# Softmax attention in one written-out order on TensorE, with the value products one step behind, rotation halves moved by DMA, and the merge's splits behind its first weights

## The chip, the cores and the metric

One Trainium2 chip, one core. Its engines run beside each other, each through its own instructions in a fixed order: TensorE (PE, matrix products), VectorE (DVE), ScalarE (ACT), GpSimd (POOL), and SyncE (SP), which issues most of the DMAs. The metric is the device time of one execution, in microseconds (us).

## The reference

Two blocks, for 512 tokens of width 1024 in fp32. The first holds two layers of feed-forward networks and token mixers. The second is one hybrid layer: from the normed input come softmax attention (8 query heads and 2 key/value heads of 128, over the 512 tokens and 256 context tokens), gated linear attention (GLA, in chunks), two sigmoid gates that merge the branches, and a squared-relu MLP. The part that the change is about:

```
qx = apply_rope(rms_norm_2(split_heads(aq, N_Q_HEADS, HEAD_DIM), q_norm), cos, sin)
kx = apply_rope(rms_norm_2(split_heads(ak, N_KV_HEADS, HEAD_DIM), k_norm), cos, sin)
...
s = jnp.einsum('bqhgd,bkhd->bhgqk', q_blk, k, preferred_element_type=jnp.float32) * (HEAD_DIM ** -0.5)
p = jax.nn.softmax(s, axis=-1).astype(v.dtype)
return jnp.einsum('bhgqk,bkhd->bqhgd', p, v)
...
y = jax.nn.sigmoid(gate_a) * (attn @ w_br_attn) + jax.nn.sigmoid(gate_g) * (gla @ w_br_gla)
return y @ w_out
```

## The kernel before

Activations lie with the features on the 128 partitions and the 512 tokens along the row. Every fp32 matrix is split into two parts that PE takes at full speed: `split` writes the high part with a cast on ACT (L182) and the low part with a subtraction on DVE (L183). A product is then three matmuls (`mm3`: low weights by high input L193, high by high L194, high by low L195). Weights come by SP's DMAs as tiles of 128 x 1024 (512 KB, `wraw`) and are split into `whi` and `wlo` just ahead of their use; in the attention there are three buffers of `wraw` and two each of `whi` and `wlo`. A projection (`proj`) is 8 such triples of 512 columns.

A scheduler orders the instructions of each engine ahead of time from its own model of time; what a buffer's last reader or writer was becomes a wait. Where the kernel marks a matmul with `pin`, its place among the marked ones is kept as written. Pools of buffers are shared by a tag: whoever takes a buffer next waits for its last user. In PSUM the attention has one buffer `pj` (projections), two `sc` of two banks each (scores), two `tp` (transposes and small sums) and one `po` (value products).

`attention_phase` follows the GLA. `query(hd)` projects one head, sums its squares over the features by matmuls (`token_sums`, PSUM name `qsum`), takes the reciprocal root on POOL, scales (`qf`), and rotates (`rotate`): four ACT copies of 32 x 512 (L1134) bring each quarter of the partitions to its partner's place (`sw`), and three DVE operations multiply by the tables and add. The two keys (`kraw`, made earlier) go the same way, their norm spread over the partitions by matmuls (`kR`). For each head and each half of the tokens come two query tiles: 6 score matmuls of 384 columns each, the maximum on DVE (L1104), its product with the norm (L1105), the exponential with its sum on ACT (L1106), the reciprocal (L1108) and the scaling (L1109) on DVE; then 12 transposes of 128 x 128 in three groups (L1117), each split into `PTh` and `PTl`; 18 value matmuls of 256 columns; and the split of their result into `ath` and `atl`. Between them stand projections for the merge's gates (`merge_gates`): the sigmoid is three ACT passes (L794 to L796), and the gate is kept in DRAM (`gsave`, L805, a DMA from ACT's queue). The scheduler alone decides how these mix, since of all this only the first matmul of a step is marked, and only in phases that use `run`.

`merge_phase` first loads the tokens' stream `x` from DRAM and scales it, splits all eight GLA heads (`gla` to `glh` and `gll`), then for 8 output tiles multiplies both branches with their weights and adds them under the gates.

Of the kernel before, what the change touches and what calls it, by code (L numbers as in the profile page):

```python
# [17 lines left out]
P = 128  # L18
D = 1024
KT = D // P  # L20
T = 512
# [127 lines left out]
class Builder:  # L149
# [554 lines left out]
    def run(self, steps):  # L704

        for step in steps:
            self.mark = True
            step()
        self.mark = False
# [87 lines left out]

    def merge_gates(self, n):
        for i in range(self.ngates, min(self.ngates + n, 2 * KT)):
            w = self.wm(self.gate_at(i))  # L800
            ps = self.psum("pj")
            self.proj(ps, w, self.hs)
            sg = self.ptmp.tile([P, T], F32, name="sg", tag="sq")
            self.sigmoid(sg, ps)
            self.nc.scalar.dma_start(self.gsave[i], sg)  # L805
            self.ngates = i + 1
# [225 lines left out]
    def attention_phase(self, ctx):  # L1032
# [7 lines left out]
        def query(hd):  # L1040
            w = self.wm(WM_AQ + hd)
            ps = self.psum("pj")
            self.proj(ps, w, self.hs)
            sq = self.ptmp.tile([P, T], F32, name="qsq", tag="sq")
            nc.scalar.activation(sq, ps, AF.Square)
            sums = self.psum("pj", "qsum")
            self.token_sums(sums, sq, 4)
            r = self.rstd(sums[:, 0:4], 4, P, "q")
            rs = self.psmall.tile([P, 4], F32, name="rs4")
            nc.vector.tensor_scalar(rs, r[:, 0:4], QSCALE, None, ALU.mult)  # L1050
            qf = p2.tile([P, T], F32, name="qf", tag="qf")
            nc.scalar.activation(qf, ps, AF.Copy, scale=self.vec("q_norm_2", 0, 1))
            qr = self.rotate(p2, qf)
            qh = p2.tile([P, T], F32R, name="qh", tag="qh")
            ql = p2.tile([P, T], F32R, name="ql", tag="ql")
            self.split(qh, ql, qr)
            return qh, ql, rs

        attn = []
        nxt = query(0)  # L1060
        for i in range(2):
            for n, at in ((C, T), (T, 0)):
                raw = self.kraw[i][:, at:at + n]
                sq = self.ptmp.tile([P, T], F32, name="ksq", tag="sq")[:, :n]
                nc.scalar.activation(sq, raw, AF.Square)
                sums = self.psum("tp", "ksum")
                self.token_sums(sums, sq, n // P)
                r = self.rstd(sums[:, :n // P], n // P, P, "k")
                R = self.psum("tp", "kR")
                self.spread(R, r, n // P)  # L1070
                kf = p2.tile([P, T], F32, name="kf", tag="qf")
                nc.scalar.activation(kf[:, :n], raw, AF.Copy, scale=self.vec("k_norm_2", 0, 1))
                if at == 0:
                    kf = self.rotate(p2, kf)
                kr = p2.tile([P, T], F32, name="kr", tag="kr", bufs=1)
                nc.vector.tensor_tensor(kr[:, :n], kf[:, :n], R[:, :n], ALU.mult)
                self.split(K[i][0][:, at:at + n], K[i][1][:, at:at + n], kr[:, :n])
        wv = [self.chunk(d["wv"][GH - 1, i]) for i in range(2)]
        self.values(wv, lambda tt, ps: self.split(Vh[:, tt], Vl[:, tt], ps), tags=("pj", "po"))
        for hd in range(8):  # L1080
            kv = hd // 4
            qh, ql, rs = nxt
            if hd < 7:
                nxt = query(hd + 1)
            oh = self.pah.tile([P, T], F32R, name=f"ath{hd}", tag=f"ah{hd}")
            ol = self.pal.tile([P, T], F32R, name=f"atl{hd}")
            for half in range(2):
                if hd and half == 0:
                    self.merge_gates(1)
                PT = [(p2.tile([P, 2, 256], F32R, name=f"PTh{i}", tag=f"PTh{i}"), p2.tile([P, 2, 256], F32R, name=f"PTl{i}", tag=f"PTl{i}"))  # L1090
                      for i in range(3)]
                probs = []
                for j in range(2):
                    qt = half * 2 + j
                    sl = slice(qt * P, (qt + 1) * P)
                    pr = p2.tile([P, 768], F32, name="probs", tag="probs", bufs=2)
                    mx = self.psmall.tile([P, 8], F32, name="mx")
                    sc = self.psum("sc", "sc", 1024).rearrange("p (e n) -> p e n", e=2)[:, :, 0:384]
                    for e in range(2):
# [170 lines left out]
```

## Time and profile before

| | |
|---|---|
| median of 3 runs | 2739.99 us (2739.67 to 2746.25) |
| the profiled execution, its own time | 2741.75 us |
| its span in the trace | 2740.0 us, 34603 instructions, mean granted clock of PE 0.997 |
| PE busy | 2698.5 us (98%), 14005 matmuls |
| DVE busy | 1532.5 us (56%) |
| ACT busy | 950.2 us (35%) |
| POOL busy | 36.1 us (1%) |
| DMA | 354.42 MB, mean 129 GB/s |

Each engine's busy time is the sum of its instructions; the share is that of the span. The execution's own time is the span and 1.75 us around it.

### The profile page before, as it was taken

Reading aid. Unit: us, or ns where it says so; the run is one execution under the profiler, and the core shown is the slowest. Engines: PE = TensorE matmul, PEld = TensorE weight load, DVE = VectorE, ACT = ScalarE, POOL = GpSimd, SP = SyncE. Lnnn points to the kernel's source line nnn. Section 1 sums busy time; section 2 is a strip of 40 time slices with the busy share of each in tenths; the row PEclk is TensorE's granted clock in tenths of the full one; section 3 lists DMA queues with packets and bytes.
Section 4 is the critical chain, followed back from the end, with each engine's and each line's share of the span. In section 5 each row is a group of like instructions: output and inputs, shape, how many; then the busy total and the mean of one; then the engine's idle time right before and its main releaser. Section 6 shows DMA issues by size and latency. Waiting matters only on the chain.

```text
span 2740.0 us, 34603 instructions
## 1 busy us (share of the span) xinstructions
PE 2698.5 (98%) x14005; PEld 2326.1 (85%) x14005; DVE 1532.5 (56%) x2499; ACT 950.2 (35%) x1474; POOL 36.1 (1%) x47
## 2 busy tenths in 40 slices
PE   7999999999999999999999999999999999999999
PEld 6888889888898888888988889899888888988887
DVE  7645567444466455754674555655446665554433
ACT  4222244222242222332432233644346652333322
POOL 0000000000000000000000000000000000000000
PEclk9999999999999999999999999999999999999999
DMA  8745543444536454433364542211221125233232
GB/s 333 246 146 185 186 138 125 145 135 135 165 114 212 138 177 150 135 100 97 111 223 138 170 146 71 89 55 47 66 85 55 51 70 176 89 100 100 93 100 78
DMA packets 102977, 354.42 MB, mean 129 GB/s; under 512 B 11424, under 2 KB 11680, under 8 KB 102688
## 3 DMA queue, kind: packets, MB, share of 16 engines
q1 hardware_dynamic: 100512, 348.00, 39.4%
q10 hardware_dynamic: 2304, 4.20, 0.4%
q8 instruction: 110, 1.80, 0.3%
q14 instruction: 51, 0.42, 0.0%
HBM read 343.76 MB, written 8.39 MB: 129 GB/s over the span
## 4 chain that ended last, share of the span: by engine, by line
PE 96%; DVE 1%; ACT 1%; DMA 1%; issue 0%; SPq 0%; POOL 0%; DVEq 0%; ACTq 0%
PE mm L193 29%; PE mm L194 29%; PE mm L195 29%; PE mm L1008 3%; PE mm L926 1%; PE mm L1014 1%; PE mm L1117 1%; ACT whi L182 0%; PE mm L446 0%; PE mm L492 0%; PE mm L479 0%; PE nR L273 0%; PE sc L1101 0%; PE sc L1103 0%; PE sc L1102 0%
## 5 line engine op out<-in xcount | busy, mean ns | idle before, releaser
L193 PE MATMUL mm<-hh,wlo 128*128 128x512 f32 (+1 forms) x2344 | 884.5, 379 | 3.2 <-ACT hh L289 1.8
L194 PE MATMUL mm<-hh,whi 128*128 128x512 f32 (+1 forms) x2344 | 878.7, 377 | 0.0
L195 PE MATMUL mm<-hl,whi 128*128 128x512 f32 (+1 forms) x2344 | 869.3, 377 | 0.4 <-DVE hl L290 0.3
L182 ACT CAST whi<-wraw 128x1024 fp32r<-128x1024 f32 (+1 forms) x443 | 456.7, 1034 | 921.6 <-PE mm L195 478.0
L183 DVE TENSOR_TENSOR wlo<-wraw,whi 128x1024 fp32r<-128x1024 f32 (+1 forms) x443 | 532.7, 1205 | 285.6 <-ACT whi L182 282.1
L193 PEld LDWEIGHTS mm<-hh,wlo 128*128 128x128 f32 x2344 | 442.8, 189 | 82.4 <-ACT hh L289 2.2
L194 PEld LDWEIGHTS mm<-hh,whi 128*128 128x128 f32 x2344 | 442.6, 189 | 77.7
L195 PEld LDWEIGHTS mm<-hl,whi 128*128 128x128 f32 x2344 | 437.4, 189 | 80.7 <-DVE hl L290 0.8
L194 PE MATMUL mm<-g,whi 128*128 128x512 f32 (+1 forms) x1147 | 416.1, 363 | 0.0
L193 PE MATMUL mm<-g,wlo 128*128 128x512 f32 (+1 forms) x1147 | 416.0, 363 | 0.0
L195 PE MATMUL mm<-g,whi 128*128 128x512 f32 (+1 forms) x1147 | 413.7, 362 | 0.0
L312 DVE SCALAR_TENSOR_TENSOR x<-mm,mod,x 128x512 f32<-128x512 f32 (+1 forms) x171 | 113.8, 666 | 319.8 <-PE mm L195 319.8
L193 PEld LDWEIGHTS mm<-g,wlo 128*128 128x128 f32 x1147 | 216.5, 189 | 33.6
L194 PEld LDWEIGHTS mm<-g,whi 128*128 128x128 f32 x1147 | 216.5, 189 | 33.5
L195 PEld LDWEIGHTS mm<-g,whi 128*128 128x128 f32 x1147 | 216.5, 189 | 33.4
L238 DVE SCALAR_TENSOR_TENSOR adaw<-adaw,cond 128x1024 f32<-128x1024 f32 x176 | 208.7, 1220 | 2.9 <-DMA adaw<-in_ada_dram 2.9
L351 DVE TENSOR_TENSOR gf<-sa,mm 128x512 f32<-128x512 f32 (+1 forms) x94 | 61.3, 653 | 197.6 <-PE mm L195 188.9
L350 ACT ACTIVATE sa<-mm 128x512 f32<-128x512 f32 (+1 forms) x94 | 53.6, 570 | 314.7 <-PE mm L195 314.7
L289 ACT ACTIVATE hh<-hn,mod 128x256 fp32r<-128x256 f32 (+1 forms) x120 | 57.9, 518 | 54.9 <-DVE hn L288 47.3
L257 DVE TENSOR_TENSOR nacc<-nacc,sq 128x256 f32<-128x256 f32 (+1 forms) x108 | 52.1, 486 | 32.5 <-ACT sq L256 31.9
L256 ACT ACTIVATE sq<-x 128x256 f32<-128x256 f32 (+1 forms) x90 | 42.0, 467 | 66.3 <-DVE x L312 64.0
L1199 DVE TENSOR_TENSOR rl<-rl 128x512 f32<-128x512 f32 (+1 forms) x36 | 22.5, 633 | 75.0 <-ACT rl L1198 74.8
(263 smaller groups left out, 2544.2 us busy)
## 6 DMA issues: line engine op xcount, KB each, us to landing
wraw<-in_ffn_in_dram SPq DMA_DIRECT2D x176, 512.0 KB, 3.5
adaw<-in_ada_dram SPq DMA_DIRECT2D x176, 512.0 KB, 4.7
wraw<-in_wm_dram SPq DMA_DIRECT2D x66, 512.0 KB, 3.7
wraw<-in_mlp_dram SPq DMA_DIRECT2D x64, 512.0 KB, 3.7
wraw<-in_ffn_out_dram SPq DMA_DIRECT2D x64, 448.0 KB, 3.4
wraw<-in_ffn_out_dram SPq DMA_DIRECT2D x32, 512.0 KB, 3.6
wraw<-in_conv_in_dram SPq DMA_DIRECT2D x24, 512.0 KB, 3.5
ads<-in_ada_dram SPq DMA_DIRECT2D x8, 512.0 KB, 10.4
```

Of the source, the lines that this page charges most:

```text
L182: self.nc.scalar.copy(hi, src)
L183: return self.nc.vector.tensor_tensor(lo, src, hi.bitcast(F32), ALU.subtract)
L193: self.pin(mm(ps, wlo, xhi, start=start, stop=False))
L194: mm(ps, whi, xhi, start=False, stop=False)
L195: mm(ps, whi, xlo, start=False, stop=stop)
L238: nc.vector.scalar_tensor_tensor(out, raw, 1.0, self.cond[:, cond], ALU.mult, ALU.mult, accum_out=dst)
L257: nc.vector.tensor_tensor(acc, acc, sq[:, :n], ALU.add)
L289: first = nc.scalar.activation(hi, u, AF.Identity, bias=sh[:, k:k + 1])
L312: self.nc.vector.scalar_tensor_tensor(x, ps[:, :seg[1]], gate[:, k:k + 1], x, ALU.mult, ALU.add)
L350: nc.scalar.activation(sa, pa[:, :seg[1]], AF.Silu)
L351: nc.vector.tensor_tensor(gf, sa, pb[:, :seg[1]], ALU.mult)
L1008: self.pin(mm(o, (xl, xh, xh)[n][:, t0:t0 + P], (hi, hi, lo)[n][:, s], start=(k == 0 and n == 0), stop=(k == KT - 1 and n == 2)))
```

## The change

`run` gets a mode (`strict`) in which every matmul of its steps is kept in the written order, and the whole attention is given to it in this mode. After an opening with the first query, the keys and the values come 16 steps, one for each head and half: the scores of step i, half a projection (`fill[0]`), the value products of step i-1, in every second step the token sums of the next query, two groups of transposes, the other half of the projection, and the third group. The projection is the next head's query in even steps up to 12 and a merge gate in the others. One more gate and the last value products end the phase. The copies of `rotate` become DMAs from ACT's queue. In the merge, the splits of the GLA heads are issued behind the last split before the first gate branch's product (`issue_after`), and the loading and scaling of `x` in the same way in the third block (m == 2) instead of at the beginning. The keys' squares are taken over all 768 columns at once, and two value tiles are summed in a score buffer.

```diff
-        self.split(hi, lo, raw)
+        self.last_split = self.split(hi, lo, raw)
...
             self.tc.keep_in_program_order(ins)
-            self.mark = False
+            self.mark = self.strict
...
         self.pin(mm(ps, wlo, xhi, start=start, stop=False))
-        mm(ps, whi, xhi, start=False, stop=False)
-        mm(ps, whi, xlo, start=False, stop=stop)
+        self.pin(mm(ps, whi, xhi, start=False, stop=False))
+        self.pin(mm(ps, whi, xlo, start=False, stop=stop))
...
+            Q.steps = self.halves(lambda: (self.wm(WM_AQ + hd), self.psum("pj")), self.hs, end)
...
+        def key_norm(i):
+            R = self.psum("sc", "kR", 1024)
+            for at, n, to, col in parts:
+                self.spread(R[:, to:to + n], kr[i], n // P, col)
...
+        def values(tts, half):
...
+                if tts[0] == 2:
+                    b = self.psum("sc", "sc", 1024)
+                    vp.update({2: b[:, 0:512], 3: b[:, 512:1024]})
...
+        Q = query(0)
+        self.run([Q.steps[0], lambda: key_sums(0), lambda: key_sums(1), Q.steps[1], lambda: key_norm(0),
+                  lambda: values((0, 1), 0), Q.sums, lambda: values((0, 1), 1), lambda: key_norm(1),
+                  *(lambda a=a, n=n: values(a, n) for a in ((2, 3), (4, 5)) for n in range(2))], True)
+        sums = []
+        for i in range(16):
+            hd, half = divmod(i, 2)
+            if half == 0 and hd < 7:
+                N = query(hd + 1)
+                fill = N.steps
+            else:
+                N, fill = None, self.gate_steps()
+            work = [lambda: scores(i, Q), fill[0]]
+            if i:
+                work.append(lambda: sum_values(i - 1))
+            self.run([*work, *sums, lambda: turn(i, (0, 1)), fill[1], lambda: turn(i, (2,))], True)
+            sums = [N.sums] if N else []
...
+        m = self.gate_steps()
+        self.run([*m, lambda: sum_values(15)], True)
         return attn
...
-            nc.scalar.copy(sw[o * 32:(o + 1) * 32], a[b * 32:(b + 1) * 32])
+            nc.scalar.dma_start(sw[o * 32:(o + 1) * 32], a[b * 32:(b + 1) * 32])
...
+            if m == 2:
+                with self.tc.issue_after(self.last_split.ins):
+                    stream()
...
+                if m == 0 and n == 1:
+                    with self.tc.issue_after(self.last_split.ins):
+                        heads()
```

What this does to the order on DVE within the attention, first before: from one head's second half, beginning with the first of two maxima (`mx<-sc`).

```order
L1104 TENSOR_REDUCE mx<-sc 128x1
L183 TENSOR_TENSOR atl_16687<-mm,ath_16686 128x256
L1105 SCALAR_TENSOR_TENSOR mx<-mx,rs_16669 128x1
L183 TENSOR_TENSOR PTl_16974<-mm,PTh_16973 128x512
L1104 TENSOR_REDUCE mx<-sc 128x1
L183 TENSOR_TENSOR PTl_16976<-mm,PTh_16975 128x512
L1105 SCALAR_TENSOR_TENSOR mx<-mx,rs_16669 128x1
L1136 TENSOR_TENSOR t_17176<-qf,rope 128x512
L183 TENSOR_TENSOR wlo<-wraw,whi 128x1024
```

And of the changed kernel: one even step (from its first maximum to the split of the value products) and the beginning of the odd step behind it, whose first row belongs to the rotation of the query projected in the even step.

```order
L1115 TENSOR_REDUCE mx<-sc 128x1
L183 TENSOR_TENSOR wlo<-wraw,whi 128x1024
L183 TENSOR_TENSOR PTl_16866<-mm,PTh_16865 128x512
L1115 TENSOR_REDUCE mx<-sc 128x1
L1116 SCALAR_TENSOR_TENSOR mx<-mx,rs_16828 128x1 x2
...
L1180 TENSOR_TENSOR t_16981<-qf,rope 128x512
L1115 TENSOR_REDUCE mx<-sc 128x1
L183 TENSOR_TENSOR wlo<-wraw,whi 128x1024
L1115 TENSOR_REDUCE mx<-sc 128x1
L183 TENSOR_TENSOR PTl_16990<-mm,PTh_16989 128x512
L1116 SCALAR_TENSOR_TENSOR mx<-mx,rs_16828 128x1
L1181 TENSOR_TENSOR sw<-sw,rope 128x512
```

In both steps a weight tile's low half now stands between the two maxima, in even steps the low half of a transposed tile as well; in odd steps the rotation's product with `sw` stands ahead of the rest of the softmax.

The end of the phase on ACT, before: from the last gate's sigmoid to the first split of a GLA head.

```order
L794 ACTIVATE sg<-mm 128x512
L182 CAST whi<-wraw 128x1024 x3
L182 CAST PTh_18235<-mm 128x512
L795 ACTIVATE sg<-sg 128x512
L182 CAST PTh_18237<-mm 128x512
L796 ACTIVATE sg<-sg 128x512
L805 DMA gsave<-sg 128x512
L182 CAST PTh_18239<-mm 128x512
L182 CAST ath_18121<-mm 128x256
L182 CAST glh_18483<-gla_13333 128x512
```

The same place of the changed kernel; between the first and the last GLA head six more like them are left out.

```order
L795 ACTIVATE sg<-mm 128x512
L182 CAST whi<-wraw 128x1024 x3
L796 ACTIVATE sg<-sg 128x512
L182 CAST ath_18278<-mm 128x256
L182 CAST glh_18480<-gla_13333 128x512
...
L182 CAST glh_18508<-gla_13340 128x512
L797 ACTIVATE sg<-sg 128x512
L806 DMA gsave<-sg 128x512
```

The casts of transposed probabilities are gone from behind the weight tiles; the sigmoid's last pass and the gate's store moved behind the eight GLA heads. On DVE at the same place, the changed kernel:

```order
L183 TENSOR_TENSOR PTl_18302<-mm,PTh_18301 128x512
L183 TENSOR_TENSOR PTl_18311<-mm,PTh_18310 128x512
L183 TENSOR_TENSOR PTl_18337<-mm,PTh_18336 128x512
L183 TENSOR_TENSOR atl_18279<-mm,ath_18278 128x256
L183 TENSOR_TENSOR wlo<-wraw,whi 128x1024 x2
L183 TENSOR_TENSOR gll_18481<-gla_13333,glh_18480 128x512
```

There the low half of the last attention output, which stood behind three weight tiles, now stands ahead of them, and the third tile behind the GLA heads.

## Rows read from the trace of the kernel before

**Rows 1.** The page: shares of the chain of work that ended last, by engine.
```profile
PE 96%; DVE 1%; ACT 1%; DMA 1%; issue 0%; SPq 0%; POOL 0%; DVEq 0%; ACTq 0%
```
**Rows 2.** Stretches: length; busy PE, PEld, DVE, ACT, POOL; clock; DMA share; GB/s.
```profile
2080.00:2240.00 160.00, 157.09 (x943) 141.76 (x942) 105.47 (x204) 100.90 (x184) 5.04 (x5) 1.00 0.15 48
2240.00:2253.00 13.00, 9.66 (x45) 8.41 (x44) 6.31 (x9) 8.11 (x14) 0.00 (x0) 0.74 0.19 46
2014.00:2253.00 239.00, 228.29 (x1372) 206.03 (x1371) 152.27 (x290) 149.40 (x269) 13.37 (x12) 0.97 0.19 60
```
**Rows 3.** PE's longer waits (start, us, instruction [idle before]), and two stretches behind them.
```profile
2016.28 0.39 PE L1008 MATMUL mm<-whi,hl 128*128 128x256 f32 x1 [1.67 <-ACT whi L182]
2060.95 0.40 PE L193 MATMUL mm<-PTh,Vl 128*128 128x256 f32 x1 [1.55 <-ACT PTh L182]
2075.52 0.50 PE L193 MATMUL mm<-hh,wlo 128*128 128x512 f32 x1 [0.82 <-DVE qm L267]
2246.00 0.58 PE L193 MATMUL mm<-PTh,Vl 128*128 128x256 f32 x1 [3.34 <-ACT PTh L182]
...
2061.30:2064.30 3.00, 3.00 (x9) 2.39 (x8) 2.35 (x5) 0.71 (x2) 0.58 (x1) 0.50 0.34 141
2075.60:2079.10 3.50, 3.50 (x16) 2.87 (x17) 3.49 (x7) 1.90 (x4) 1.49 (x1) 1.00 0.57 154
```
**Rows 4.** Timeline of PE: starts of neighbouring matmuls of each width.
```profile
2236.09 0.39 PE L195 MATMUL mm<-hl,whi 128*128 128x512 f32 x1
2236.32 0.39 PE L193 MATMUL mm<-hh,wlo 128*128 128x512 f32 x1
...
2056.16 0.34 PE L1102 MATMUL sc<-Kh,qh 128*128 128x384 f32 x1
2056.34 0.34 PE L1103 MATMUL sc<-Kl,qh 128*128 128x384 f32 x1
...
2234.45 0.28 PE L194 MATMUL mm<-PTh,Vh 128*128 128x256 f32 x1
2234.57 0.28 PE L195 MATMUL mm<-PTl,Vh 128*128 128x256 f32 x1
...
2057.80 0.82 PE L1117 MATMUL mm<-ident,probs 128*128 128x128 f32 x6
2058.45 0.95 PE L261 MATMUL qsum<-mhalf,qsq 128*128 128x1 f32 x8
```
**Rows 5.** Timeline of DVE: a maximum of a second tile, its scaling, and the next maximum.
```profile
2052.07 0.95 DVE L1104 TENSOR_REDUCE mx<-sc 128x1 f32<-128x768 f32 x1
2055.48 0.62 DVE L1109 TENSOR_SCALAR probs<-probs,mx 128x768 f32<-128x768 f32 x1
2056.72 0.96 DVE L1104 TENSOR_REDUCE mx<-sc 128x1 f32<-128x768 f32 x1 [0.62 <-PE sc L1103]
```
**Rows 6.** Groups by line, 2080 to 2240 us: busy, mean ns | idle before.
```profile
L183 DVE TENSOR_TENSOR PTl<-mm,PTh 128x512 fp32r<-128x512 f32 x40 | 26.7, 684 | 10.4 <-ACT PTh L182 10.4
L183 DVE TENSOR_TENSOR wlo<-wraw,whi 128x1024 fp32r<-128x1024 f32 x13 | 15.9, 1221 | 2.5 <-ACT whi L182 2.5
L182 ACT CAST whi<-wraw 128x1024 fp32r<-128x1024 f32 x13 | 13.7, 1055 | 0.0
L1134 ACT COPY sw<-qf 32x512 f32<-32x512 f32 x20 | 12.4, 618 | 0.3
L794 ACT ACTIVATE sg<-mm 128x512 f32<-128x512 f32 x9 | 5.5, 609 | 2.6 <-PE mm L195 2.6
```
**Rows 7.** Timelines of ACT and DVE at the end of the phase.
```profile
2242.54 2.92 ACT L182 CAST whi<-wraw 128x1024 fp32r<-128x1024 f32 x3
2251.56 4.28 ACT L182 CAST glh<-gla 128x512 fp32r<-128x512 f32 x8
2249.11 3.49 DVE L183 TENSOR_TENSOR wlo<-wraw,whi 128x1024 fp32r<-128x1024 f32 x3
```
**Rows 8.** The tile gsave: issues (duration ns min/median/max) and landing.
```profile
L805 ACTq DMA_DIRECT2D gsave<-sg x10: 326/326/327, 2087.0 to 2247.5; - x10
DMA to landing us min/median/max: 2.0/2.7/6.8
```

More of the change, by code (lines that the diff above doesn't have):

```diff
@@ L702, in gla_phase, with run @@
                   tail[6], m[2], tail[7], m[3], tail[8]])
-    def run(self, steps):
+    def run(self, steps, strict=False):
+        self.strict = strict
         for step in steps:
@@ L796, in sigmoid @@
         act(out, out, AF.Exp, scale=-1.0)
[L798 to L806, printed above, removed]
     def gate_steps(self):
@@ L1040, in query @@
         def query(hd):
[L1041 to L1070, printed above, removed]
+            Q = SimpleNamespace()
@@ new lines, in end @@
+            def end(ps):
+                Q.sq = self.ptmp.tile([P, T], F32, name="qsq", tag="sq")
+                nc.scalar.activation(Q.sq, ps, AF.Square)
+                qf = p2.tile([P, T], F32, name="qf", tag="qf")
+                nc.scalar.activation(qf, ps, AF.Copy, scale=self.vec("q_norm_2", 0, 1))
+                qr = self.rotate(p2, qf)
+                Q.h = p2.tile([P, T], F32R, name="qh", tag="qh")
+                Q.l = p2.tile([P, T], F32R, name="ql", tag="ql")
+                self.split(Q.h, Q.l, qr)
@@ new lines, in turn @@
+        def turn(i, groups):
+            for g in groups:
+                hi = p2.tile([P, 2, 256], F32R, name=f"PTh{g}", tag=f"PTh{g}")
+                lo = p2.tile([P, 2, 256], F32R, name=f"PTl{g}", tag=f"PTl{g}")
+                PT[i, g] = hi, lo
+                ps = self.psum("tp")
+                for a in range(2):
+                    for j in range(2):
+                        kt = 2 * g + a
+                        o = a * 256 + j * P
+                        self.pin(nc.tensor.transpose(ps[:, o:o + P], probs[i][j][:, kt * P:(kt + 1) * P], self.ident))
+                self.split(hi.rearrange("p a q -> p (a q)"), lo.rearrange("p a q -> p (a q)"), ps)
@@ new lines, in sum_values @@
+        def sum_values(i):
+            hd, half = divmod(i, 2)
+            if not half:
+                attn.append((self.pah.tile([P, T], F32R, name=f"ath{hd}", tag=f"ah{hd}"), self.pal.tile([P, T], F32R, name=f"atl{hd}")))
+            po = self.psum("po")[:, 0:256]
+            vs = slice((hd // 4) * P, (hd // 4 + 1) * P)
+            for kt in range(6):
+                hi, lo = PT[i, kt // 2]
+                self.mm3(po, Vh[:, kt, vs], Vl[:, kt, vs], hi[:, kt % 2], lo[:, kt % 2], kt == 0, kt == 5)
+            s = slice(half * 256, (half + 1) * 256)
+            self.split(attn[hd][0][:, s], attn[hd][1][:, s], po)
@@ L1144, in merge_phase, with heads, stream @@
         self.px = self.pool(self.ctx, "x2", side="right", reuse_waits="tile")
[L1145 to L1150 removed]
         mp = self.pool(ctx, "merge", 1, reuse_waits="tile")
         gs = []
[L1153 to L1157 removed]
+        def heads():
+            for i in range(KT):
+                gh = mp.tile([P, T], F32R, name=f"glh{i}")
+                gl = mp.tile([P, T], F32R, name=f"gll{i}")
+                self.split(gh, gl, gla[i])
+                gs.append((gh, gl))
+        def stream():
+            self.x_tiles(self.xsave)
+            R1 = self.psum("sm", "fR1")
+            for seg, r in zip(SEGS, self.r1):
+                self.spread(cut(R1, seg), r, seg[1] // P)
+            for k in range(KT):
+                nc.vector.scalar_tensor_tensor(self.x[k], self.x[k], self.vec("final_g", k, 1), R1, ALU.mult, ALU.mult)
         ys = []
```

130 lines of the change are left out of this document (64 added, 66 removed).

## Prediction, before any run of the changed kernel

> **What bounds the kernel now.** I read the chain that ended last first: TensorE (PE) holds 96% of it [rows 1], and the change leaves its matmuls the same in number and shape. So a gain can only be idle PE time or half-speed clock taken back, a loss only such time added. By the order of instructions PE does the same as before up to the end of the gated linear attention (the last nR spread, 2014 us) and again from the first weights of the merge on (2253 us); everything in question lies in these 239 us.
>
> The view by stretches says what is lost there today: PE is busy 228.29 of 239 us at a mean clock of 0.97 [rows 2], so 10.7 us idle and, since a stretch at 0.97 costs 3% of its time, about 7 us of clock: **17 us in all**. The 160 us of steady attention lose only 2.9 of it at full clock; the last 13 us lose 3.3 idle plus 0.26 × 13 = 3.4. The rest lies at the start. The single waits show which gaps also cost clock: behind a gap of 1.55 us PE runs at a granted clock of 0.50 (the level of 1.2 GHz) for 3 us and more, while one of 0.82 us is followed by 1.00 [rows 3]; the 3.34 us gap lies in the stretch at 0.74. So a gap costs its length, and one of the longer ones some 1.7 us more (some 3.4 us at half speed).
>
> **The change part by part. PE's step.** The new order is written out in 16 equal steps: scores, half a projection, the value products of the step before, transposes, the other half, last transposes. From the distances of starts of neighbouring matmuls (0.23 at 512 columns, 0.175 at 384, 0.12 at 256, 0.11 per transpose) [rows 4] I get: scores 12 × 0.175 = 2.1; a half 12 × 0.227 = 2.7; value products 18 × 0.119 = 2.15; transposes 0.87 and 0.44; the next query's token sums, in odd steps, 0.95. Between the end of the scores and the first transposes PE has 2.7 + 2.15 = **4.86 us** of other work, 5.8 in odd steps. The transposes need both tiles' probabilities, and the old trace prices that chain: the second tile's maximum begins at 2052.07, the second scaling ends at 2055.48 + 0.62, **4.03 us** later; the maximum itself begins 0.2 us after PE has moved on from the scores (2056.34 + 0.18 to 2056.72) [rows 5]. 4.2 against 4.86 looks covered. It is, if the second maximum starts at once, and the order on VectorE (DVE) says it doesn't.
>
> **Even steps.** Between the two maxima stand now the low half of a weight tile (1.22 us) and the split of the last transposes (0.68) [rows 6]. On DVE a following instruction starts about 0.08 before the busy time ends (three weight tiles of 1.22 take 3.49 together [rows 7]). Zero is where PE leaves the last half: transposes to 0.44, scores of tile 0 to 1.49, of tile 1 to 2.54. DVE: first maximum 1.69 to 2.56; weight tile to 3.70 (its cast on ScalarE, ACT, is over by 0.2 + 0.61 + 1.06 = 1.9 [rows 6], so not late); split to 4.31; second maximum only now, 1.6 us after its scores. 4.31 + 4.03 = 8.34, transposes at 8.35; PE stands ready at 2.54 + 2.72 + 2.15 = 7.40. **Stall 0.95, 7 times: 6.6 us.** Bounds: 0.6 if PE's own distances run at 0.235 and 0.13, 1.2 if ACT's other work delays an exponential.
>
> **Odd steps** follow a query, so its rotation stands in there too. Ahead of the first maximum comes qf × rope: qf is ready at 1.42 (its square and its copy, taken as 0.6 each like the sigmoid's first pass of the same size), so the maxima run 2.03 to 2.90 and, behind the weight tile, 4.04 to 4.91; split to 5.5. Next in DVE's order, ahead of the second tile's bias (so of the second exponential) and of both scalings, stands sw × rope. The four ACT copies that fed it cost 0.62 us each, 20 of them 12.4 us in the steady stretch [rows 6]; ACT is not the bound, so their removal gives nothing by itself. In their place are four DMAs from ACT's queue, issued from 2.35 to 2.8 (behind the cast of a weight tile and of the transposes), 0.33 us each by the only DMA of that queue in the trace, so the last starts at 3.35 to 3.8. That row's transfers (256 KB; the new ones carry 64 KB) land after 2.0 / 2.7 / 6.8 us [rows 8]; no row shows 64 KB. I take the median: sw lands at 6.05 to 6.5, then 0.61 for the product, the bias, the second exponential, and the scaling that ends near 9.3 to 9.6, against PE ready at 8.30. **Stall 1.2 (0.95 at a landing of 2.0 us), 7 times: 8.4 us.** A landing of 6.8 would make it 5.3. The last step has no such work and doesn't stall. Steady loss: **15 us**, where 2.9 stood.
>
> The Trainium skill ("DMA: Bandwidth & Descriptors", section "Anatomy of one DMA — SWDGE (gpsimd) path") gives a DMA a fixed 2.0 us or so plus bytes over 436 GB/s, an estimate of 2.15 us for 64 KB. The fastest landing of the row, 2.0, fits such a fixed part, the median doesn't. By the page's figure an odd step would stall 0.95 and the sum would be about 1.8 us lower. It speaks against this change all the same, as the fixed part outlasts the copies.
>
> **Start.** The wait for the first weights (1.67 us [rows 3]) stays, as they are cast and split no earlier; for it and the step to the low halves, since the order now begins with a projection's both halves, I take 2.5, and 1.7 of clock. New: the values of token blocks 2 and 3 use the score buffer in which the first key's spread norms lie, and wait until the rotated key has been multiplied by them. Counted from the end of the first query's projection PE arrives there after two spreads of 1.3, 48 value matmuls of 0.119 and 0.95 of sums, at 9.3. The chain is longer: query copies 1.9 to 2.8; four issues and a landing (1.0 + 2.7); two products 1.3; a cast 0.5; again 1.0 + 2.7; three products 1.85: 12.9 to 13.8 at the median, 11.2 with both landings 2.0. Stall 1.9 to 4.5; I take 3.4, with a drop of 1.7. Step 0 has no value products as cover and its first maxima stand behind a weight tile and the last value splits: transposes at 7.1, PE ready at 4.9, 2.2 more. **Start: 11.5 us.** Before: 17 − 2.9 − 6.7 = 7.5.
>
> **End.** Today ACT casts three weight tiles (2.92 us) ahead of the last probabilities, and that is the 3.34 us wait [rows 3, 7]. The new order puts the last value products behind the last gate, so that wait goes. What is late next: on DVE the last output's low half stands ahead of the merge's first weight tile; ACT reaches its high half after the sigmoid's first pass, three casts and a second pass, 4.6 us after the gate; so the tile is ready at 4.6 + 0.35 (half the 0.68 of a split) + 1.14 = 6.1, PE (value products 2.15, a spread 0.95) at 3.1: 3.0 idle and a drop of 1.7. Then the splits of the GLA heads, now behind the first gate weights' cast: eight casts (4.28 us [rows 7]) stand ahead of the last sigmoid pass, whose store must land before the next weight tile, laid over its buffer, can be written: 9.3 + 2.0 to 2.7 + 1.2 = 12.6 to 13.3, PE there at 6.1 + 5.5 = 11.6: 1.0 more, as the slow clock hides a part. **End: 5.7**, where 6.7 stood. The stream tiles loaded at the third block instead of the first have free time on either side: nothing; without that cover its eight scalings would stand once in DVE's way, ahead of those splits.
>
> **Sum.** 11.5 + 15.0 + 5.7 = 32.2 against 17: **+15 us**. Against the profiled execution's own 2741.75 (span 2740.0) that is 2757; the median of the runs is 1.8 lower, so the time predicted is **2755**.
>
> **The rivals.** (a) *As worked out:* 2755, with the bounds of the terms (even 0.6 to 1.2, odd 0.95 to 1.9, start 9 to 14, end 4 to 8) 2746 to 2766: chance 0.62. (b) *The cover holds; not slower.* If the second maximum began by 3.3 instead of 4.31, the transposes would come by 7.40 and the 14 stalls be gone: 2755 − 15 = 2740. For it: 4.86 of cover against 4.03 + 0.2; PE's distances in the new mix may be longer than in the rows, and every 0.1 in the cover takes 1.4 us from the sum. Against it: DVE's order is fixed, with 1.7 us of work between the maxima. If the start's stall failed as well, 2735. Chance 0.18. (c) *Each stall costs clock too.* The stalls lie between 0.82 us (no drop) and 1.55 (drop) [rows 3]. Were every one followed by 3.4 us at half speed: 14 × 1.7 = 24 more, 2779. For it: the odd stalls of 1.2 lie nearer to 1.55. Against: the even ones lie nearer to 0.82. Odd ones alone: 2767. Chance 0.13. (d) *The rotation lands late.* At the row's slowest landing, 6.8, the odd stall is 5.3: 7 × 4.1 = 29 more, 2784. Against it: a quarter of the bytes and DMA engines 15% busy [rows 2]. Chance 0.07. That the change doesn't do what it says is excluded: PE's rows stand as written.
>
> **How the numbers follow.** The range takes in most of (a), (b) down to 2737 and (c) for the odd steps: 2737 to 2776; left out are about half of (c), (d) and a third of (b), 0.2 together. 0.3% is 8 us, about what a measurement can tell from no change: faster needs under 2732, which only (b) with more than the start gained gives: 0.08. The same: the rest of (b) and (a)'s low tail: 0.22. Slower: 0.70.
>
> **What would show it.** The profile after should have, in each even step, a PE wait of about 1 us ahead of the first transposes, released by DVE's scaling; in odd steps one of 1.2, with sw × rope on DVE waiting for a DMA; a wait of 2 to 4 us ahead of the value matmuls into the score buffer; no wait for transposed probabilities at the end, and one of 3 us for the merge's first weight tile. The granted clock stays at 1.0 in the steady part. The prediction is wrong if DVE's second maximum follows its scores at once, if landings differ much from 2.7, or if gaps near 1 us drop the clock.

## The result and the profile after

The changed kernel takes 2766.93 us (median of 4 runs, 2765.85 to 2771.84), the kernel before 2742.82 in the same comparison (4 runs, 2739.67 to 2746.25): a ratio of **1.0092**, interval 1.008 to 1.0104. It is slower by 24 to 25 us, where 15 were forecast.

The profiled execution has a span of 2765.5 us. The page's chain has moved from PE to the engines that feed it (compare [rows 1]):

```profile
PE 93%; DVE 3%; ACT 1%; DMA 1%; issue 1%; ACTq 0%; SPq 0%; POOL 0%; DVEq 0%
```

The view by stretches: the opening, step 0, steps 1 to 15, the end, and all of it (columns as in [rows 2]).

```profile
2018.00:2059.00 41.00, 32.74 (x201) 30.17 (x200) 18.01 (x31) 12.06 (x21) 4.09 (x3) 0.83 0.37 116
2059.00:2075.60 16.60, 14.72 (x82) 12.97 (x81) 7.99 (x14) 5.99 (x11) 0.00 (x0) 0.90 0.20 64
2075.60:2258.00 182.40, 171.85 (x1026) 153.53 (x1024) 120.03 (x235) 97.94 (x178) 8.86 (x7) 1.00 0.20 60
2258.00:2283.00 25.00, 20.66 (x99) 16.86 (x99) 5.61 (x9) 13.26 (x22) 0.00 (x0) 0.93 0.37 127
2018.00:2283.00 265.00, 239.96 (x1404) 213.54 (x1402) 151.64 (x287) 129.25 (x231) 12.95 (x10) 0.96 0.24 75
```

PE is idle for 25.0 of 265 us, and the clock takes 0.17 × 41 + 0.10 × 16.6 + 0.07 × 25 = 10.4 more: 35 us. The kernel before lost 17.5 in its 239 us by the same count (10.7 idle, and half of the 13.7 us that its trace has at half speed); the prediction has 17. A measure that needs no such sum: from the start of the last spread of the GLA (nR) to the span's end the kernel before takes 2740.0 − 2013.55 = 726.45 us, the changed one 2765.5 − 2018.10 = 747.40. **The attention and what follows cost 20.95 us more.** The other 4.55 us of the two spans lie ahead of that spread, in code that the change doesn't touch: over the fourteen traces of this study it starts between 2011.95 and 2018.85 us, early and late in kernels of either family. That part varies from one execution to the next, and nothing here is explained by it. The medians differ by 24 us and the lengths by 21; what the other 3 us are, no trace tells.

PE's waits (start, us, instruction [idle before]): the opening's, step 0's, one even and one odd step, the end's.

```profile
2021.66 0.50 PE L193 MATMUL mm<-hh,wlo 128*128 128x512 f32 x1 [2.51 <-DVE wlo L183]
2047.06 0.55 PE L999 MATMUL sc<-whi,hl 128*128 128x256 f32 x1 [4.28 <-DVE kr L1076]
2056.63 0.74 PE L999 MATMUL sc<-wlo,hh 128*128 128x256 f32 x4 [1.46 <-DVE Vl L183]
2069.14 0.30 PE L1133 MATMUL mm<-ident,probs 128*128 128x128 f32 x1 [1.21 <-ACT probs L1117]
2096.57 0.96 PE L1133 MATMUL mm<-ident,probs 128*128 128x128 f32 x7 [0.67 <-DVE probs L1120]
2109.38 0.85 PE L1133 MATMUL mm<-ident,probs 128*128 128x128 f32 x6 [0.70 <-DVE probs L1120]
2274.29 0.47 PE L193 MATMUL mm<-ath,wlo 128*128 128x512 f32 x1 [2.94 <-DVE wlo L183]
2282.59 0.50 PE L193 MATMUL mm<-glh,wlo 128*128 128x512 f32 x1 [0.96 <-DVE wlo L183]
```

Steps 1 to 15 have a wait of 0.67 to 0.71 us ahead of the second transpose; step 13 alone differs, with 0.70 ahead of the first and 0.43 ahead of the second. The first transpose needs tile 0 only; it is shown 0.30 long where it takes 0.11 in a row of its kind, so a step loses some 0.87. DVE in an even step:

```profile
2089.80 0.96 DVE L1115 TENSOR_REDUCE mx<-sc 128x1 f32<-128x768 f32 x1 [2.79 <-PE sc L1114]
2090.68 1.22 DVE L183 TENSOR_TENSOR wlo<-wraw,whi 128x1024 fp32r<-128x1024 f32 x1
2091.81 0.68 DVE L183 TENSOR_TENSOR PTl<-mm,PTh 128x512 fp32r<-128x512 f32 x1
2092.41 0.95 DVE L1115 TENSOR_REDUCE mx<-sc 128x1 f32<-128x768 f32 x1
...
2095.81 0.62 DVE L1120 TENSOR_SCALAR probs<-probs,mx 128x768 f32<-128x768 f32 x1
```

The second maximum starts 2.61 us behind the first, as the prediction had it (1.69 to 4.31), and the scaling ends 4.02 us later (4.03 in [rows 5]). The rotation in an odd step, DMAs on ACT's queue and the product on DVE, and below it the tile's own view:

```profile
2101.51 1.18 ACTq L1178 DMA_DIRECT2D sw<-qf  x2
2102.72 1.25 ACTq L1178 DMA_DIRECT2D sw<-qf  x2
2105.65 0.68 DVE L1181 TENSOR_TENSOR sw<-sw,rope 128x512 f32<-128x512 f32 x1
```
```profile
L1178 ACTq DMA_DIRECT2D sw<-qf x32: 514/612/1089, 2034.5 to 2227.6; - x32
DMA to landing us min/median/max: 1.9/2.0/6.3
```

DVE does not wait for it here. The opening, DVE's waits for rotated halves and what stood behind them:

```profile
2044.78 0.69 DVE L1181 TENSOR_TENSOR sw<-sw,rope 128x512 f32<-128x512 f32 x1 [0.27 <-DMA sw<-kf]
2046.23 0.69 DVE L1076 TENSOR_TENSOR kr<-t,kR 128x512 f32<-128x512 f32 x1
2054.10 0.69 DVE L1181 TENSOR_TENSOR sw<-sw,rope 128x512 f32<-128x512 f32 x1 [3.85 <-DMA sw<-kf]
2056.16 0.42 DVE L183 TENSOR_TENSOR Vl<-sc,Vh 128x256 fp32r<-128x256 f32 x1
```

The first key's rotated half lands at 2044.7, its product `kr` ends at 2046.9 and frees the score buffer: PE goes on at 2047.06. The second key's lands at 2054.1. Behind its three products stands the split of a value tile, which reads the score buffer that PE's next matmuls write: two value tiles share that buffer, and the second one's last matmuls wait until the first one's split is done. These four transfers landed late, 6.0 us behind their issue (median; the tile's own view above has 2.0 for all), while the DMA engines were busy at a share of 0.94, most of it with weight tiles (the stretch with the columns of [rows 2], and the issues from 2046 to 2049 us):

```profile
2047.00:2051.00 4.00, 3.94 (x18) 3.97 (x19) 2.23 (x4) 1.02 (x2) 0.00 (x0) 0.50 0.94 333
sw<-kf ACTq DMA_DIRECT2D x4, 64.0 KB, 6.0
```

Two stretches of the opening, one with the keys' sums and one behind it (columns as in [rows 2]):

```profile
2026.10:2028.80 2.70, 2.70 (x26) 2.69 (x25) 0.17 (x1) 0.00 (x0) 0.96 (x1) 1.00 0.75 308
2029.20:2032.40 3.20, 3.20 (x9) 2.45 (x9) 0.00 (x0) 0.00 (x0) 1.31 (x1) 0.50 0.00 0
```

PE waits for nothing in either, and yet the second runs at the lower clock; PE's last wait ended at 2021.66, 7 us ahead of it. The end, on ACT and DVE (compare [rows 7]):

```profile
2268.84 2.93 ACT L182 CAST whi<-wraw 128x1024 fp32r<-128x1024 f32 x3
2272.20 0.36 ACT L182 CAST ath<-mm 128x256 fp32r<-128x256 f32 x1
2272.59 0.42 DVE L183 TENSOR_TENSOR atl<-mm,ath 128x256 fp32r<-128x256 f32 x1 [8.87 <-ACT ath L182]
2272.93 1.21 DVE L183 TENSOR_TENSOR wlo<-wraw,whi 128x1024 fp32r<-128x1024 f32 x1
2281.31 1.23 DVE L183 TENSOR_TENSOR wlo<-wraw,whi 128x1024 fp32r<-128x1024 f32 x1 [7.16 <-DMA gsave<-sg]
```

### The profile page after: what moved, and what is told of

Its sections match the earlier page's. It is cut to its first block, busy times and chain, and to the rows that moved or that the text cites. A ratio compares the mean times of both kernels' runs of the same rounds, so it can differ in the third digit from the quotient of the medians.

```text
span 2765.5 us, 34644 instructions
## 1 busy us (share of the span) xinstructions
PE 2710.8 (98%) x14005; PEld 2333.5 (84%) x14005; DVE 1531.9 (55%) x2497; ACT 927.2 (34%) x1432; POOL 35.6 (1%) x45
## 4 chain that ended last, share of the span: by engine, by line
PE 93%; DVE 3%; ACT 1%; DMA 1%; issue 1%; ACTq 0%; SPq 0%; POOL 0%; DVEq 0%
PE mm L193 28%; PE mm L194 28%; PE mm L195 28%; PE mm L999 3%; PE mm L917 1%; PE mm L1133 1%; DVE wlo L183 1%; PE mm L1005 1%; PE mm L446 0%; PE mm L492 0%; ACT probs L1117 0%; PE nR L273 0%; DVE probs L1120 0%; PE mm L479 0%; PE nsum L261 0%
## 6 DMA issues: line engine op xcount, KB each, us to landing
ads<-in_ada_dram SPq DMA_DIRECT2D x8, 512.0 KB, 10.2
```

## The experiments

**Theory A**, from the prediction and this trace: the time goes where DVE's order, fixed ahead of time, puts other work between a product and the one that PE waits for (the weight tile between the maxima; the last output's split ahead of the merge's weights), and where the opening strings three rotations one behind the other. **Rival B**: the DMAs of the rotation themselves make the steps wait. **Rival C**: 4.9 us of cover are too short, whatever the order.

All runs in one table. "From nR" is the span less the start of the last nR spread, from the trace, and its difference to 726.45. It comes from one trace each; the two traces of the changed kernel differ by 5.7 us in it. The ratio is to the runs of the kernel before on the same chip.

| kernel | median us (runs) | ratio (interval) | from nR |
|---|---|---|---|
| changed kernel | 2766.93 (4) | 1.0092 (1.0080 to 1.0104) | 747.40, +20.95 |
| the same once more | 2770.64 (1) | | 753.12, +26.67 |
| maxima first | 2751.57 (6) | 1.0034 (1.0020 to 1.0047) | 736.00, +9.55 |
| rotation by copies | 2759.85 (4) | 1.0072 (1.0055 to 1.0089) | 743.36, +16.91 |
| merge as before | 2776.62 (4) | 1.0124 (1.0105 to 1.0143) | 755.68, +29.23 |
| values swapped | 2764.15 (4) | 1.0088 (1.0067 to 1.0108) | 747.45, +21.00 |
| keys first | 2763.86 (4) | 1.0078 (1.0061 to 1.0094) | 749.70, +23.25 |
| end mended | 2768.76 (4) | 1.0095 (1.0078 to 1.0113) | 752.27, +25.82 |
| all three mended | 2744.62 (11) | 1.0009 (1.0000 to 1.0018) | 726.74, +0.29 |
| all three, with copies | 2745.29 (12) | 1.0013 (1.0004 to 1.0021) | 730.45, +4.00 |
| all three, copies in the opening | 2744.62 (11) | 1.0005 (0.9995 to 1.0014) | 725.06, −1.39 |
| before, rotation by DMA | 2746.97 (10) | 1.0018 (1.0009 to 1.0027) | 730.06, +3.61 |
| before, merge part | 2743.64 (10) | 1.0003 (0.9994 to 1.0013) | 725.25, −1.20 |

**Maxima first.** `scores` remembers the second tile's bias; the split of the next weight tile, that of the last transposes and the rotation's products are issued behind it.

```diff
-        self.last_split = self.split(hi, lo, raw)
+        if self.strict and self.behind is not None:
+            with self.tc.issue_after(self.behind.ins):
+                self.last_split = self.split(hi, lo, raw)
...
+            with self.tc.issue_after(bias.ins):
+                for f in late:
+                    f()
```

> The changed kernel, with DVE's order within a step mended: both maxima and their products with the norm come ahead of the weight tile's low half, the last transposes' split and the query's rotation. Theory A (DVE's order starts the second maximum 1.7 us late, and this is the wait of 0.67 to 0.70 us, 0.86 to 0.90 counted from matmul to matmul, ahead of the transposes in all 16 steps): even steps lose their wait, odd ones keep 0.2 at most; 11 to 13 us faster than the changed kernel, near 2755. Theory B (the odd steps wait for the rotation's DMAs, or ACT's queue of them delays the exponentials): odd steps keep 0.9, about 6 us faster, 2761. Theory C (the 4.9 us of cover are too short whatever DVE's order): all keep most of it, within 3 us of 2767.

Theory A holds, B and C fall: of the waits in steps 1 to 15 a single one over 0.3 us is left (0.44, in step 13), PE is busy for 162.94 of 165 us, and the length falls by 11.4. The edit moves three things at once (the weight tile, the transposes' split, the rotation's products); what each is worth alone was not run. DVE in an even step, and the stretch of the steps:

```profile
2083.37 0.96 DVE L1127 TENSOR_REDUCE mx<-sc 128x1 f32<-128x768 f32 x1
2084.25 0.28 DVE L1128 SCALAR_TENSOR_TENSOR mx<-mx,rs 128x1 f32<-128x1 f32 x2
2084.44 0.68 DVE L187 TENSOR_TENSOR PTl<-mm,PTh 128x512 fp32r<-128x512 f32 x1
2085.04 1.22 DVE L187 TENSOR_TENSOR wlo<-wraw,whi 128x1024 fp32r<-128x1024 f32 x1
```
```profile
2071.00:2236.00 165.00, 162.94 (x983) 146.77 (x982) 113.50 (x225) 93.66 (x170) 9.30 (x7) 1.00 0.21 64
```

**Rotation by copies**, the one line of `rotate` undone.

> The changed kernel with the rotation's halves moved by ACT copies again. Theory A: the steps' waits stay as they are (0.67 to 0.70), since in the trace sw had landed when DVE came to it; at the start two DMA rounds of about 4 us each (four issues of 0.6 and a landing of 2.0) become 2.5 us of copies, so the 4.28 us wait ahead of the value matmuls into the score buffer falls to 1 or 2 and with it a clock drop: 3 to 7 us faster, near 2762. Theory B (rotation by DMA makes the odd steps wait): these lose 0.9 each, 6 us more, near 2756. If moving the halves by DMA was worth anything to the steps: slower than 2767.

4.0 us less. The steps' waits stand as they were (0.67 to 0.71 in each), so B is out for them; the gain is the opening's:

```profile
2041.75 0.55 PE L999 MATMUL sc<-whi,hl 128*128 128x256 f32 x1 [3.33 <-DVE kr L1076]
2049.43 0.74 PE L999 MATMUL sc<-wlo,hh 128*128 128x256 f32 x4 [0.92 <-DVE Vl L183]
```

The wait for the buffer fell less than expected, to 3.33 and not to 1 or 2: the four copies of a rotation take 2.50 us in this trace and still run one behind the other. The second key's wait fell from 1.46 to 0.92, 6.8 us less run at half speed in the opening and step 0, and 1.5 us are lost again at the end, where the second wait grew from 0.96 to 2.45. That wait, for the landing of the last gate's store, lies between 0.96 and 3.00 in the traces that have this end, and at 0.96 and 1.53 in the two of the unchanged kernel; this edit need not be what moved it.

**Merge as before**: `stream()` and `heads()` called ahead of the loop, no `issue_after`.

> The changed kernel with the merge phase as before: the GLA heads' splits and the scaling of x are written ahead of the first weights again. Theory A (the end's waits are the last attention output's split ahead of the first weight tile on DVE and the last gate's store): DVE now does 8 splits of 0.61 and 8 scalings of about 0.65 ahead of that tile, so the 2.94 us wait becomes about 12 and the 0.96 us one goes: 8 to 10 us slower, near 2776. Rival (the merge part of the change costs what it saves): within 2 us of 2767.

8.3 us more. PE's wait for the first weight tile, and what now stands ahead of that tile on DVE (the first rows of eight splits and eight scalings):

```profile
2277.56 0.77 PE L193 MATMUL mm<-ath,wlo 128*128 128x512 f32 x1 [13.21 <-DVE wlo L183]
...
2266.11 1.90 DVE L183 TENSOR_TENSOR gll<-gla,glh 128x512 fp32r<-128x512 f32 x3
2267.92 2.72 DVE L1204 SCALAR_TENSOR_TENSOR x<-x,vecs,fR 128x512 f32<-128x512 f32 x4
```

So the merge part of the change mends what the new end of the attention would cost; it is no gain over the kernel before, as its own run below shows.

**Values swapped.** The value tiles of blocks 4 and 5 ahead of 2 and 3.

```diff
-                  *(lambda a=a, n=n: values(a, n) for a in ((2, 3), (4, 5)) for n in range(2))], True)
+                  *(lambda a=a, n=n: values(a, n) for a in ((4, 5), (2, 3)) for n in range(2))], True)
```

> The changed kernel with the values of token blocks 4 and 5 ahead of those of 2 and 3 at the start. Theory A (the 4.28 us wait is for the score buffer, held by the first key's spread norms until the rotated key is multiplied): the buffer is wanted 5.7 us later, that wait is gone with its 6.8 us of half clock, and no more than 1 us waits for the two other buffers; 5 to 8 us faster, near 2760. Rival (something else is late there, such as the value weights): the wait moves to the matmuls that now come first, within 2 us of 2767.

The 4.28 us wait and its half clock are gone, 1.10 waits in its place; but the wait for the second key's products grew from 1.46 to 3.12. The opening and step 0 together are 6.3 us shorter, as expected. The length is the same all the same, because steps 1 to 15 took 4.9 us more in this trace, with a late rotation in one of them (below), and the end's second wait grew to 3.00. The total tells nothing of the gain.

**Keys first.** Both keys' sums ahead of the first query, the first key's spread between its halves.

```diff
-        self.run([Q.steps[0], lambda: key_sums(0), lambda: key_sums(1), Q.steps[1], lambda: key_norm(0),
+        self.run([lambda: key_sums(0), lambda: key_sums(1), Q.steps[0], lambda: key_norm(0), Q.steps[1],
```

> The changed kernel with another opening: both keys' token sums ahead of the first query's projection, and the first key's spread between its halves. Theory A (the opening loses time because the key's two DMA rounds begin behind the first query, and because PE has nothing to do while the first weights are split): the sums, 2.73 us long, fill the 2.51 us wait; the rotated key is ready before the value matmuls want its score buffer, so the 4.28 us wait, 6.8 us of half clock and most of the 1.46 us one go; 8 to 12 us faster, near 2757. Rival (the buffer waits for something else): the 4.28 us wait stays, at most 3 us faster.

A miss in size. The buffer's wait is gone, as A has it; but the sums themselves wait 1.47 us, the first value tiles 1.27 (ACT comes late to the first query), and for the second key's product PE waits 3.33. With the clock (10.2 us at half speed, 17 in the changed kernel) and step 0 the loss fell from 18.6 to 13.0, by 5.6 and not by 8 to 12. The total shows none of it: in this trace steps 1 to 15 took 5.2 us more, with a late rotation among them, and the end's second wait grew to 1.98, with a clock drop.

**End mended.** The last value products between the last gate's halves, and the GLA heads' splits behind that gate's store.

```diff
-        self.run([*m, lambda: sum_values(15)], True)
+        self.run([m[0], lambda: sum_values(15), m[1]], True)
...
+                    with self.tc.issue_after(self.last_split.ins), self.tc.issue_after(self.last_gate.ins):
```

> The changed kernel with another end: the last value products between the halves of the last gate, and the GLA heads' splits behind the store of that gate. Theory A (at the end PE waits 2.94 us for the merge's first weight tile, since on DVE the last output's split stands ahead of it, and 0.96 us for the store under the third tile): the output's split is done before the weights are cast, the first wait becomes 1.5 to 2.2 (less cover on PE now), the second goes; 1.5 to 4 us faster, near 2764. Rival (the weight tile is late because of its own cast or transfer): both waits stay or the first grows by 2.15, the cover moved away; same or 2 us slower.

The first wait fell as expected:

```profile
2275.09 0.50 PE L193 MATMUL mm<-ath,wlo 128*128 128x512 f32 x1 [1.99 <-DVE wlo L183]
```

The one of 0.96 is gone, and a new one of 0.34, for the low half of a GLA head, has come. From step 15's wait to the end the trace is 2.0 us shorter than the first. The total shows nothing of it, since here too steps 1 to 15 took 5.6 us more, with a late rotation among them, and the opening with step 0, which this edit doesn't touch, 1.3 us more.

**All three mended.**

> The changed kernel with the three mended orders together: maxima first, keys first, end. If the waits are of separate causes, the gains add: 11.4 in the steps as measured, 8 to 12 at the opening, 1.5 to 4 at the end, so 21 to 27 off the 20.7 us by which the changed kernel's attention is longer: 2734 to 2742, the same as the kernel before or just faster. If one wait only hides another: 2745 to 2755.

+0.29 against +20.95: the gains add up, and the kernel is about where the one before is. The median of 2744.62 lies 2.6 above the range that was expected, 3 above the 2741.47 of the kernel before on that chip. The second key's wait remains:

```profile
2049.97 0.74 PE L1003 MATMUL sc<-wlo,hh 128*128 128x256 f32 x4 [2.87 <-DVE Vl L187]
```

Opening, step 0, steps, end (compare the stretches above):

```profile
2017.00:2056.00 39.00, 33.40 (x231) 31.04 (x230) 18.87 (x32) 12.49 (x21) 4.09 (x3) 0.91 0.36 115
2056.00:2070.00 14.00, 12.85 (x70) 11.11 (x70) 8.64 (x16) 6.86 (x13) 0.00 (x0) 1.00 0.31 85
2070.00:2242.00 172.00, 170.22 (x1027) 152.97 (x1026) 118.11 (x235) 97.34 (x176) 9.30 (x7) 1.00 0.21 63
2242.00:2262.00 20.00, 17.77 (x85) 14.79 (x84) 5.51 (x8) 12.40 (x20) 0.00 (x0) 0.91 0.51 164
```

**All three, with copies**, and **copies in the opening** alone (the keys and the first query).

> The changed kernel with the three mended orders and the rotation's halves moved by ACT copies again, so that of the change the written order, the value products behind and the merge part remain. Theory A (the 2.87 us wait that the three mended orders left at the opening is for the second key's rotated halves, which land 4.6 us behind their last issue; and now and then a step's halves land 2 us late, with a clock drop behind): that wait falls under 1, no step has a wait above 0.7; 3 to 5 us faster than with the DMAs, 2738 to 2742. Rival (the copies hold ACT where casts of weights or exponentials wait behind them): the wait stays or others of about 0.5 appear in odd steps; same or up to 4 slower.

> The three mended orders, with ACT copies for the rotation of the keys and the first query and DMAs for that of the other queries. Theory A (at the opening the rotation's latency is on the path, so copies are better there by 2 us; in the steps the copies hold ACT and cost 0.46 us in each odd step, so DMAs are better there): no wait above 1.5 at the opening and none of 0.46 in the steps; 2 to 5 us faster than the mended orders with copies alone, 1 to 3 faster than those with DMAs alone, 2740 to 2744. Rival (the two differ by chance): within 1 us of both in the attention's length.

Copies take the opening's 2.87 us wait to 0.92, as expected; but in odd steps they bring a wait of 0.46 ahead of the transposes (x7), as the rival had it. In these two traces the opening takes 1.9 us less with the copies, the steps 4.0 more and the part from the merge's first product on 1.6 more, so that the length is 3.7 more, not 3 to 5 less: in the steps the DMAs are better. With each where it is better no wait of 0.46 is left, one of 0.58 stands in step 13, and the length is 1.39 under that of the kernel before. The times don't tell these three versions apart, their intervals overlap; the last is the same as the kernel before (1.0005, interval 0.9995 to 1.0014). No version here beats it.

**Before, rotation by DMA**, and **before, merge part**: one part of the change alone in the kernel before.

> The kernel before with one part of the change alone: the rotation's halves by DMA from ACT's queue. Theory A (ACT's copies are off the path that sets the end, and the DMAs' four issues hold ACT's queue about as long as the copies took, 0.61 us each): no gain in the steady part; at the opening the keys come later by some 1.5 us a round: between no change and 4 us slower, 2740 to 2744. Rival (freeing ACT of 20 us of copies lets the scheduler's order run better): 2 to 5 us faster.

> The kernel before with the merge part of the change alone: GLA heads' splits behind the first gate branch's weights, x loaded and scaled in the third block. Theory A (in the kernel before the scheduler had put three weight tiles ahead of those splits anyway, and the merge part only matters with the new end of the attention, where without it 13.2 us are lost): no change, 2739 to 2743. Rival (it is worth what it is named for in either): 3 us faster or more.

The rotation by DMA alone costs 3.6 us in the length and 0.18% in the times (5 us, interval above 1), a little more than the 4 expected at most. It is not the price of the DMAs alone: in this kernel the scheduler decides the order, and with the edit it orders PE's, DVE's and ACT's instructions of the attention otherwise (at the end PE waits 3.11, 1.50 and 0.76 us for transposed probabilities, where the kernel before has the one wait of 3.34). The merge part alone does nothing that the times show.

**The changed kernel once more.**

> The changed kernel once more, unchanged, for a second trace. Theory A: the waits of the opening, the 16 steps and the end come again within 0.5 us, and so does the length of the attention (20.7 us more than before); what varies by up to 5 us is the time ahead of the attention, in code that the change doesn't touch, by where the clock is low. If a step's rotated halves land late as in three other traces, one or two steps wait 2 to 2.6 us and the clock drops behind. Rival (the opening's extra loss was chance): it falls from 18 to 12 us.

Two of the opening's waits come again (2.51, 4.04); the second key's is 3.02 where it was 1.46, outside the 0.5 expected, with a shorter clock drop ahead of it, and opening and step 0 together take the same time. The steps' waits come to within 0.02 but for step 11's, the end's first at 2.94 and its second at 1.53. The length is 5.7 more, and most of it lies in step 11, the rotation of the seventh head's query. Its last two issues on ACT's queue, and DVE's wait:

```profile
2199.80 2.25 ACTq L1178 DMA_DIRECT2D sw<-qf  x2
...
2205.58 0.69 DVE L1181 TENSOR_TENSOR sw<-sw,rope 128x512 f32<-128x512 f32 x1 [2.76 <-issue]
```

PE's wait there becomes 2.30 us with half clock behind it; step 13 has a smaller one, also with a drop. In four of the six traces that have the changed kernel's steps and DMAs (values swapped, keys first, end mended, and this one) step 11 waits 2.3 to 2.6 us, and steps 1 to 15 take 4.9 to 5.6 us more than in the first trace; in that one the two issues took 1.73 us and DVE waited 0.20. In the two traces with copies in the steps it does not occur.

These two issues are slow in all nine traces that have DMAs in the written-out steps, 1.73 to 2.61 us where those of other steps take 1.16 to 1.45; with maxima first, where the rotation's products stand later on DVE, PE waits nothing for them in step 11, though they took 2.40 us there. And the traces show what coincides. Beside the queues of data the page lists DMA queues of the kind `instruction`; one of them, q8, moves 16 KB at a time. Such a transfer begins beside these issues:

```profile
q8 instruction: 1, 0.02, 8.9%
sw<-qf ACTq DMA_DIRECT2D x2, 64.0 KB, 3.1
```

(This is 2199.5 to 2200.5 us; 3.1 is the median landing, where it is 2.0 at the same place of step 9.) Over the ten traces with DMAs for the rotation, 17 of 388 such issues took 0.87 to 1.97 us, nine at step 11 and eight in the opening. At each of the 17 a q8 transfer began between 0.61 us before the issue's start and 0.05 behind it; at none of the other 371, which took 0.69 at most, did one. That the one delays the other is not shown: no run moves these transfers.

## Why the prediction was right and wrong

**The direction and the steps** were right. 15 steps at 0.87 are 13, where 15.0 stood for 14. The even steps went by the chain as worked out, 0.67 + 0.19 against 0.95. Maxima first took the wait away, so it was DVE's order. Two sizes in the odd steps were off and met in the middle: an issue takes 0.6 us, not 0.33, and lands 2.0 us later, not 2.7, so that sw × rope came at 5.54 us from the step's zero, not at 6.05 to 6.5, and had no wait; 0.89 instead of 1.2. The wait for a DMA that the forecast had in the odd steps did not occur; what is left there is DVE's order, so that this term came out near partly by luck. The Trainium skill ("DMA: Bandwidth & Descriptors", section "Anatomy of one DMA — SWDGE (gpsimd) path") gave an estimate of 2.15 us for the 64 KB, by a fit for DMAs that GpSimd issues; the median landing of 2.0 for these, from ACT's queue, agrees with it. The larger transfer's 2.7 [rows 8], which I took, did not fit. That the fixed part outlasts the copies was wrong as it stood: 2.0 is less than four copies of 0.62, and only issues and landing together are more. That the last step would not stall was wrong: it splits the last gate's weight tile like the others.

**The step that failed is the term "Start: 11.5 us".** By the same count it measured 18.6: 2.51 and 1.7 of clock as forecast; 4.28 for the score buffer (3.4 taken) with 6.8 us at half speed (3.4 lost, 1.7 taken); and three things that the sum didn't have: 1.7 for a second stretch at half speed, behind the keys' sums; 1.46 for a value tile's split behind the second key's rotation; 1.7 of clock in step 0, whose waits of 1.21 and 0.68 were near the 2.2 taken. The second trace of the same kernel gives 18.2. I had followed the first key's chain and stopped there; the second key's comes behind it on the same `sw` buffer and the same two queues, a third round, and its halves landed 5.3 to 6.3 us behind their issue, where I had counted 2.0 to 2.7 for a landing. Values swapped and keys first took the first key's wait away, as that reading asks, but the second key's wait grew to 3.12 and 3.33, and all three mended orders left 2.87 of it. Only the copies brought it to 0.92. That these landings are late because weight tiles fill the DMA engines is read from their share of 0.94 and was not run by itself. Why the clock fell behind the keys' sums stays open.

**The end**, 5.7, measured 2.94 + 0.96 + 1.7 = 5.6, with both causes as worked out. The second wait and the opening's last one were both at the low end here: 0.96 to 3.00 and 1.46 to 3.02 over the traces with the same end and the same opening, so that 5.6 lies this near 5.7 in part by chance. The losses of the kernel before were 17.5, near the 17 taken. So the sum should have read 18.6 + 13 + 5.6 = 37 against 17.5, +20, and the length shows 20.95.

**What lies outside the sum.** The median against which the change was measured is 2742.82, not 2739.99, and the profiled executions differ by 4.55 us ahead of the attention for no reason of the change. The late rotation, rival (d), is real, at step 11 and a little at step 13, and not in every execution; steps 1 to 15 take some 5 us more where it occurs. Whether it is part of the untraced runs' times isn't known. Rival (c) did not happen: the steps' waits drop no clock, at 0.7 us each. Rival (b) is refuted by the trace of the steps, and maxima first shows the condition under which it would have been true.

## What to carry to other kernels

Where one engine's order is written by hand, the others' are not: look for what a scheduler puts between two instructions that feed one waiting consumer, and price the pair from the second one. A cover of 4.9 us for a chain of 4.2 is enough only if nothing of 0.7 us can slip in. And follow a shared buffer through all its users at the start of a phase; the last of three in a row is the late one.

## What the hardware showed that I had not expected

The token sums, 24 matmuls of one column in 2.73 us with no wait between them, are followed by a stretch at a granted clock of 0.50 (1.2 GHz), though PE had waited for nothing in the 7 us ahead of it: here the clock fell without a gap. And gaps of the same length, 1.2 us and then 0.7 in step 0, were followed by half speed in the first trace and by full speed in that of the copies (columns as in [rows 2], the clock third from the end), so here a gap's length alone doesn't tell:

```profile
2070.20:2073.40 3.20, 3.20 (x12) 2.81 (x13) 1.39 (x2) 1.17 (x2) 0.00 (x0) 0.50 0.02 5
2063.00:2066.40 3.40, 3.40 (x19) 2.93 (x20) 1.29 (x2) 1.07 (x2) 0.00 (x0) 1.00 0.02 5
```

A DMA of 32 x 512 between places in SBUF held ACT's queue for 0.51 to 1.09 us for the queries of the first trace, where the store of 128 x 512 to DRAM held it for 0.33 [rows 8].
